# A hybrid decoder step on one core: the delta rule's norms as column scalars, and other first transfers

## The chip, the cores and the metric

The kernel runs on one core of a Trainium2 chip. A core has five engines that work at the same time and meet at semaphores: TensorE (PE: matmuls and transposes into PSUM; its weight loads are shown apart, as PEld), VectorE (DVE), ScalarE (ACT), GpSimd (POOL) and SyncE (SP), which here issues nearly all DMA transfers. Each engine takes its instructions strictly in the order in which they stand. The metric is the device time of one execution, in microseconds (us); lower is better.

## The reference, cut to what matters

One layer for 512 prompt rows and 8 x 4 sample rows of width 1024. Both kinds are modulated by a condition, multiplied by one wide projection (11280 columns), and go through two branches, windowed attention and a gated delta rule, which are merged at the end. The change touches the delta rule of the prompt rows (8 heads, head width 128):

```python
q = l2norm(q) * (B_HEAD_DIM ** -0.5)
k = l2norm(k)                                  # l2norm(t) = t * rsqrt(sum(t*t) + 1e-6)
...
cum = jnp.cumsum(g, axis=-1)
decay = jnp.exp(jnp.where(causal, cum[..., :, None] - cum[..., None, :], -jnp.inf))
kk = jnp.einsum('bhid,bhjd->bhij', k, k)
lower = jnp.where(strict, beta[..., :, None] * kk * decay, 0.0) + jnp.eye(n)
rhs = jnp.concatenate([beta[..., None] * v, beta[..., None] * k * jnp.exp(cum)[..., None]], axis=-1)
sol = lax.linalg.triangular_solve(lower, rhs, left_side=True, lower=True, unit_diagonal=True)
u, w = sol[..., :B_HEAD_DIM], sol[..., B_HEAD_DIM:]
v_new = u - jnp.einsum('bhid,bhde->bhie', w, state)
qk = jnp.einsum('bhid,bhjd->bhij', q, k) * decay
out = (q * exp(cum)) @ state + qk @ v_new
new_state = exp(cum[-1]) * state + (k * exp(cum[-1] - cum)).T @ v_new
...
ob = ob * lax.rsqrt(jnp.mean(ob * ob, axis=-1, keepdims=True) + NORM_EPS)   # after the rule, per row
```

It also returns the caches of keys and values, moved on by four rows (`kv*_s`, copied from input to output).

## The kernel before, in words

The kernel is written as a Python program that records operations, and a planner on the host, a list scheduler with rough costs for each engine, orders them before anything runs. All recorded operations are issued from one line of the program (L745 of the profile, L748 after the change), so the profile tells them apart by their tiles. What sets the order around the change: the order in which the code records, ranks, the earliest time `at` that a transfer may be planned, the costs in `Recorder.cost`, and the table `NUDGES`, which shifts margins in stretches of operations by seeded random numbers. Where the planner sees TensorE without work it puts in a placeholder, a matmul of ones (`warm<-ones`).

The front. `cT` (the conditions) and `bT` come in; `cs` is their silu. For each of the eight row tiles k: a block `wm[k]` of 1 MB is multiplied with `cs` (`pd<-wm,cs`), ScalarE copies the sum to `Y`, a product with the selection `selc` puts scale and shift into columns (`pd<-cst,Y`), VectorE applies them to `xT[k]`, and ScalarE and VectorE split the result into two rounded parts `hhi` and `hlo`; the weights `wf[k]` of the first three column tiles are split likewise (`whi`, `wlo`). The products of these three (`pp`, `pg`, `pb<-hhi,whi` and so on) run tile by tile behind it. `cst` is a block of constants (identity, `selc`, masks).

The stream. Then come 85 column tiles (`stream`, one `Job` each): 512 KB of weights (`wt`), split into `hi` and `lo`, three rounded products each, in two halves of 272 columns, in one of two PSUM banks (`pp`). ScalarE empties a bank (for the delta branch into `ext` and `cx`, the short convolution follows as `acc`). Between these products the planner lays the small work of attention and of the delta rule.

The delta rule of one head, `delta_blocks(h)` and, for two heads at once, `delta_rule(p)`. For four chunks of 128 rows: `NTs` is the decay, `cr` the exponent of the running sum as a row on all partitions, `rc` a tile of columns with one number a row of the chunk; `rc[:, 0]` becomes the reciprocal norm of k, `rc[:, 1]` that of q (times the scale). Before the change the norms are also needed along the free dimension: `rc` is transposed on TensorE (`pb<-cst,rc`), copied (`rrow`), written to DRAM (`dr`) and read back as two tiles `rb` with the same row on all partitions, and `QKd`, `NTs` and `cr` are multiplied with them. `NTs` then holds the lower matrix, `QKd` the products of q and k, `kr` the rows of k, `vr` those of v. Diagonal blocks of `NTs` go through DRAM (`dblk`) to `Ls`, are inverted into `Tb`, and go through `dtz` to `Tc`. `S` is the state, `vn` the new values, `z` the right side less the state's part.

The copies of the caches are 168 transfers of 496 or 512 KB from DRAM to DRAM (`moves`), which the planner may place at times spread evenly from 48 to 850 us.

Of the kernel before, what the change touches and what calls it, by code (L numbers as in the profile page):

```python
# [37 lines left out]
MOVES = (48.0, 850.0)  # L38
# [231 lines left out]
class Recorder:  # L270
# [103 lines left out]
    def cost(self, op, args):  # L374
# [23 lines left out]
        elif e == "ve":  # L398
# [8 lines left out]
            if op.name == "scalar_tensor_tensor" and pointer or op.name == "transpose":  # L407
                c += 0.055
            op.cost, op.late = c - 0.08, 0.08
        elif e == "se":  # L410
            c = (0.155 if in_psum else 0.21) + 0.83e-3 * n
            a = (0.07 if "accum_out" in op.kw else 0.0) + (0.08 if pointer else 0.0)
# [385 lines left out]
def body(ctx, tc, io):  # L798
# [27 lines left out]
    def pb_():  # L826
        return psb.tile([128, 512], F32, name="pb", tag="b")
# [67 lines left out]
    with ExitStack() as fctx:  # L895
        fr = pool(fctx, "front", 1)
        cT = fr.tile([128, KT, 9], F32, name="cT")
        sp.dma_start(cT, io["cT"])
        bT = fr.tile([128, 24], F32, name="bT")
        se.dma_start(bT, io["bT"])  # L900
# [11 lines left out]
        for k in range(KT):  # L912
            sp.dma_start(wm[k], io["w_mod"][k])
            if k == 0:
                sp.dma_start(cst, io["const"])
# [3 lines left out]
        rec.front = False  # L919
        sp.dma_start(wab, io["w_ab"])  # L920
# [9 lines left out]
        for k in range(KT):  # L930
# [3 lines left out]
            with rec.together():  # L934
                for i in range(KT):
                    q = i % 4
                    pe.matmul(pc[32 * q:32 * q + 32, 0:256], cs[:, i, :], wm[k][:, i, :], start=(i < 4), stop=(i >= 4),
                              tile_position=(0, 32 * q))
# [3 lines left out]
            for u in range(2):  # L942
                pe.matmul(pv[:, u, 0:9], Y[:, 128 * u:128 * u + 128], C("selc"), start=True, stop=True)
# [10 lines left out]
            ve.tensor_scalar(h[:, :SEQ], h[:, :SEQ], m[:, 1, 0:1], m[:, 0, 0:1], op0=OP.mult, op1=OP.add)  # L954
# [1491 lines left out]
```

## Time and profile before

| | us |
|---|---|
| median of three runs | 890.68 (887.01 to 891.37) |
| the profiled execution | 890.4 |
| its span in the profile | 888.6 |
| TensorE (PE) busy | 871.0 (98%) |
| VectorE (DVE) busy | 714.8 (80%) |
| ScalarE (ACT) busy | 431.8 (49%) |
| DMA, mean over the span | 272 GB/s |

The span is the time from the first instruction to the last; the execution's own time is 1.8 us longer. Busy means that an instruction is recorded on the engine; a placeholder of TensorE counts as busy, and matmuls that run at a lower clock do as well. The clock of TensorE that was granted is given as a share of its full speed. A row of the profile names the written tile, an arrow, and the tiles read, with buffer numbers left out.

### The profile page before, as it was taken

The numbers are of one execution on the slowest core, as the hardware profiler recorded it, in microseconds if no ns is written. First come the engines' busy times: TensorE is split into PE (matmuls) and PEld (weight loads), VectorE is DVE, ScalarE is ACT, GpSimd is POOL, SyncE is SP. The second block draws the span as 40 slices with busy tenths as digits, with TensorE's granted clock in tenths as the row PEclk, the third lists the DMA queues.
The fourth block names the chain that finished last, engine by engine and source line by source line (L and its number), as shares of the span: only waits on it lengthen the run. The fifth ranks groups of instructions, "written<-read, shape, count | busy, mean of one in ns | idle before, by whom it ended". The sixth has DMA issues, their size and how long they took to land.

```text
span 888.6 us, 20372 instructions
## 1 busy us (share of the span) xinstructions
PE 871.0 (98%) x7868; PEld 825.9 (93%) x7868; DVE 714.8 (80%) x1599; ACT 431.8 (49%) x1059; POOL 40.7 (5%) x115
## 2 busy tenths in 40 slices
PE   8999999999999998999999999999999999999996
PEld 7899999999998998997999999999999999997876
DVE  2678657777759989998999999777889889957657
ACT  2476645685544765444784644564531223234431
POOL 0030000010000000001000000011010000000000
PEclk8999999999999999999999999999999999999998
DMA  9786676557787788899687889479899999989983
GB/s 354 291 222 204 212 225 222 189 169 226 227 267 237 234 245 256 279 306 317 210 261 261 268 266 299 160 234 422 267 292 364 355 357 417 416 257 322 324 324 126
DMA packets 105796, 241.74 MB, mean 272 GB/s; under 512 B 32138, under 2 KB 59228, under 8 KB 101988
## 3 DMA queue, kind: packets, MB, share of 16 engines
q1 hardware_dynamic: 105556, 240.43, 80.2%
q8 instruction: 62, 1.02, 0.4%
q14 instruction: 34, 0.28, 0.1%
q10 hardware_dynamic: 144, 0.01, 0.0%
HBM read 223.79 MB, written 104.29 MB: 369 GB/s over the span
## 4 chain that ended last, share of the span: by engine, by line
PE 87%; DVE 4%; ACT 4%; DMA 2%; issue 1%; SPq 1%; POOL 1%; DVEq 0%; ACTq 0%; POOLq 0%
PE pp L745 65%; PE pg L745 9%; PE pd L745 9%; PE pb L745 3%; ACT L745 1%; DMA wm<-in_w_mod 1%; DMA wv<-dw 1%; DVE acc L745 1%; SPq L745 1%; DVE ya L745 1%; PE warm L745 0%; DVE NB L745 0%; ACT ext L745 0%; DVE XF L745 0%; POOL q L745 0%
## 5 line engine op out<-in xcount | busy, mean ns | idle before, releaser
L745 PE MATMUL pp<-hhi,hi 128*128 128x272 f32 x1360 | 399.5, 294 | 3.2 <-ACT cx L745 2.7
L745 PE MATMUL pp<-hlo,hi 128*128 128x272 f32 x1360 | 399.9, 294 | 0.0
L745 PE MATMUL pp<-hhi,lo 128*128 128x272 f32 x1360 | 399.5, 294 | 0.0
L745 PEld LDWEIGHTS pp<-hhi,hi 128*128 128x128 f32 x1360 | 257.1, 189 | 4.4 <-ACT cx L745 2.9
L745 PEld LDWEIGHTS pp<-hlo,hi 128*128 128x128 f32 x1360 | 257.4, 189 | 2.2 <-issue 1.4
L745 PEld LDWEIGHTS pp<-hhi,lo 128*128 128x128 f32 x1360 | 256.8, 189 | 1.5 <-issue 0.8
L745 ACT ACTIVATE hi<-wt 128x1024 fp32r<-128x1024 f32 (+1 forms) x101 | 103.6, 1026 | 166.3 <-PE pp L745 138.6
L745 DVE TENSOR_TENSOR lo<-wt,hi 128x1024 fp32r<-128x1024 f32 (+1 forms) x101 | 118.8, 1176 | 34.5 <-ACT hi L745 34.2
L745 DVE SCALAR_TENSOR_TENSOR acc<-ext,cw,acc 128x568 f32<-128x568 f32 x72 | 57.2, 801 | 5.9 <-ACT acc L745 5.4
L745 ACT ACTIVATE P<-P,st 128x256 f32<-128x256 f32 (+1 forms) x64 | 31.3, 491 | 34.5 <-DVE st L745 34.2
L745 DVE TENSOR_TENSOR slab<-slab 128x512 f32<-128x512 f32 (+1 forms) x66 | 42.9, 666 | 0.0
L745 DVE TENSOR_REDUCE slab<-slab 128x8 f32<-128x512 f32 (+2 forms) x66 | 42.4, 653 | 0.2
L745 ACT ACT_TABLE_LOAD x32 | 41.1, 1283 | 1.8 <-PEq L2419 1.2
L745 ACT ACTIVATE zt<-pp 128x272 f32<-128x272 f32 x48 | 18.7, 389 | 38.8 <-PE pp L745 33.4
L745 PE MATMUL pp<-ybh,hi 128*128 128x272 f32 x128 | 36.9, 288 | 0.0
L745 PE MATMUL pp<-ybh,lo 128*128 128x272 f32 x128 | 36.9, 288 | 0.0
L745 PE MATMUL pp<-ybl,hi 128*128 128x272 f32 x128 | 36.8, 288 | 0.0
L745 ACT ACTIVATE q<-pp 64x272 f32<-64x272 f32 (+1 forms) x48 | 26.2, 545 | 17.4 <-PE pp L745 16.9
L745 PE MATMUL pg<-k,q 128*128 128x128 f32 (+1 forms) x192 | 33.7, 307 | 0.4 <-DVE PT L745 0.4
L745 PEld LDWEIGHTS pg<-k,q 128*128 128x128 f32 x192 | 27.6, 190 | 2.8 <-issue 1.1
L745 DVE TENSOR_TENSOR tmp<-Ls,Tb 32x15 f32<-32x15 f32 (+7 forms) x120 | 23.1, 193 | 7.5 <-DMA Ls<-dblk 3.3
L745 DVE CUSTOM_DVE_ANT_0 P<-pg,bias 128x256 f32<-128x256 f32 (+1 forms) x64 | 24.0, 401 | 5.0 <-PE pg L745 4.5
(404 smaller groups left out, 1571.5 us busy)
## 6 DMA issues: line engine op xcount, KB each, us to landing
out_kv_s<-in_cache SPq DMA_DIRECT2D x144, 512.0 KB
wt<-in_w_in SPq DMA_DIRECT2D x85, 512.0 KB
out_kv_s<-in_cache SPq DMA_DIRECT2D x24, 496.0 KB
wm<-in_w_mod SPq DMA_DIRECT2D x8, 1024.0 KB
slab<-in_ks SPq DMA_DIRECT2D x32, 256.0 KB
slab<-in_vs SPq DMA_DIRECT2D x32, 256.0 KB
kv<-in_ks SPq DMA_DIRECT2D x16, 512.0 KB
kv<-in_vs SPq DMA_DIRECT2D x16, 512.0 KB
```

The costliest lines, as they stand in the source:

```text
L745: getattr(real[x.engine], x.name)(*map(arg, x.args), **{k: arg(v) for k, v in x.kw.items()})
```

## The change

The matrix of the triangular system and the products are brought to another basis by a diagonal matrix of k's norms. What was a factor on rows and on columns becomes a factor on rows alone, which is a column of scalars and needs no broadcast along the free dimension. `vr` is scaled by half the norm (`rc[:, 5]`, a second square root), `vn` by `beta` over the norm, and the outputs by q's reciprocal norm where ScalarE reads them. The transpose, `rrow`, `dr`, `rb` and the three multiplications go.

At the front `cT`, `bT` and `selc` come in one transfer `c0`; the first weights come in two halves, multiplied in two groups; `cst` comes behind the front; the first scaling of `xT` is done in two halves; and the weights of column tile 5, which were planned at time 0, are planned from 28 us on (`BEHIND`) as those of tiles 3 and 4 are. The cache copies are placed at times that reach 78% by 600 us, 95% by 800 and the last by 850. Two costs of the planner are altered, and `NUDGES` has other numbers.

```diff
-MOVES = (48.0, 850.0)
+MOVES = (48.0, 600.0, 800.0, 850.0), (0, 0.78, 0.95, 1)
...
 NUDGES = (
-    (0, 9912, 1047), (572, 972, 696727), (6242, 7442, 352100), (4626, 5026, 884219), (8230, 9430, 221759),
+    (0, 9881, 1023), (3823, 5023, 22586), (5072, 6272, 796932), (9467, 9507, 754021), (7424, 7824, 95492),
...
@@ cost
+            far = lambda v: v.ix.ndim > 1 and v.ix.shape[-1] > 1 and abs(int(v.ix.reshape(v.ix.shape[0], -1)[0, 1]) - int(v.ix.flat[0])) > 4
+            if n > 64 and any(far(v) for v in views if size(v) > 1):
+                c += 0.72e-3 * n
...
-            a = (0.07 if "accum_out" in op.kw else 0.0) + (0.08 if pointer else 0.0)
+            a = (0.015 if "accum_out" in op.kw else 0.0) + (0.08 if pointer else 0.0)
...
@@ front
-        cT = fr.tile([128, KT, 9], F32, name="cT")
-        sp.dma_start(cT, io["cT"])
-        bT = fr.tile([128, 24], F32, name="bT")
-        se.dma_start(bT, io["bT"])
+        c0 = fr.tile([128, 72 + 24 + 9], F32, name="c0")
+        sp.dma_start(c0, io["c0"])
+        cT, bT, selc = c0[:, 0:72].rearrange("p (k b) -> p k b", b=9), c0[:, 72:96], c0[:, 96:105]
...
         for k in range(KT):
-            sp.dma_start(wm[k], io["w_mod"][k])
-            if k == 0:
-                sp.dma_start(cst, io["const"])
+            for i in range(0, KT, KT if k else 4):
+                j = slice(i, KT if k else i + 4)
+                sp.dma_start(wm[k][:, j], io["w_mod"][k][:, j])
...
         rec.front = False
+        sp.dma_start(cst, io["const"])
...
-            with rec.together():
-                for i in range(KT):
-                    q = i % 4
-                    pe.matmul(pc[32 * q:32 * q + 32, 0:256], cs[:, i, :], wm[k][:, i, :], start=(i < 4), stop=(i >= 4),
-                              tile_position=(0, 32 * q))
+            for j in range(0, KT, KT if k else 4):
+                with rec.together():
+                    for i in range(j, KT if k else j + 4):
+                        q = i % 4
+                        pe.matmul(pc[32 * q:32 * q + 32, 0:256], cs[:, i, :], wm[k][:, i, :], start=(i < 4), stop=(i >= 4),
+                                  tile_position=(0, 32 * q))
...
-                pe.matmul(pv[:, u, 0:9], Y[:, 128 * u:128 * u + 128], C("selc"), start=True, stop=True)
+                pe.matmul(pv[:, u, 0:9], Y[:, 128 * u:128 * u + 128], selc, start=True, stop=True)
...
-            ve.tensor_scalar(h[:, :SEQ], h[:, :SEQ], m[:, 1, 0:1], m[:, 0, 0:1], op0=OP.mult, op1=OP.add)
+            for w in (slice(0, HF), slice(HF, SEQ)) if k == 0 else [slice(0, SEQ)]:
+                ve.tensor_scalar(h[:, w], h[:, w], m[:, 1, 0:1], m[:, 0, 0:1], op0=OP.mult, op1=OP.add)
...
@@ stream
-                    jobs[x].load(raws[x]).at = 0.0 if i else BEHIND
+                    jobs[x].load(raws[x]).at = 0.0 if i > 2 else BEHIND
...
@@ delta_blocks
-        rc = dl.tile([128, 5, 4], F32, name="rc")
+        rc = dl.tile([128, 6, 4], F32, name="rc")
...
+        se.activation(rc[:, 5], rc[:, 0], AF.Sqrt, bias=eps1[:, 0:1], scale=0.25)
         se.activation(rcf[:, 0:8], rcf[:, 0:8], AF.Sqrt, bias=eps4[:, 0:1])
         ve.reciprocal(rcf[:, 0:8], rcf[:, 0:8])
         ve.tensor_scalar(rc[:, 1], rc[:, 1], qscale, None, op0=OP.mult)
-        pn = pb_()
-        pe.transpose(pn[0:8, 0:128], rcf[:, 0:8], ident)
-        rrow = dl.tile([8, 128], F32, name="rrow", bufs=1)
-        ve.tensor_copy(rrow, pn[0:8, 0:128])
-        dr = dram.tile([8, 128], F32, name=f"dr{h}")
-        sp.dma_start(dr, rrow)
-        rb = dl.tile([128, 4, 128], F32, name="rb0", tag="vr"), dl.tile([128, 4, 128], F32, name="rb", bufs=1)
-        for a in range(2):
-            sp.dma_start(rb[a].rearrange("p c i -> p (c i)"),
-                         dr[4 * a:4 * a + 4].rearrange("a b -> (a b)")[None, :].to_broadcast([128, 512]))
-        for i, t in ((2, beta), (3, necum), (4, tail)):
+        for i, t in ((3, beta), (4, tail)):
             ve.tensor_mul(rc[:, i], rc[:, 0], t[:, h:32:8])
+        ve.tensor_mul(rc[:, 2], rc[:, 0], rc[:, 3])
         yield 1.0
-        ve.tensor_mul(QKd, NTs, rb[1])
-        ve.tensor_mul(NTs, NTs, rb[0])
-        ve.tensor_mul(cr, cr, rb[1].rearrange("p c i -> p (c i)"))
...
+                ve.scalar_tensor_tensor(QKd[:, c, :], pkv[:, cc, 1, :], rc[:, 0, c:c + 1], NTs[:, c, :],
+                                        op0=OP.mult, op1=OP.mult)
                 ve.scalar_tensor_tensor(NTs[:, c, :], pkv[:, cc, 0, :], rc[:, 2, c:c + 1], NTs[:, c, :],
                                         op0=OP.mult, op1=OP.mult)
-                ve.scalar_tensor_tensor(QKd[:, c, :], pkv[:, cc, 1, :], rc[:, 0, c:c + 1], QKd[:, c, :],
-                                        op0=OP.mult, op1=OP.mult)
-            yield 3.0 if c2 else 14.0
+            yield 3.0
...
-        se.activation(vr, cols128(pt), AF.Copy, scale=0.5)
+        for c in range(4):
+            se.activation(vr[:, c], cols128(pt)[:, c], AF.Copy, scale=rc[:, 5, c:c + 1])
...
@@ delta_rule
-                    ve.scalar_tensor_tensor(z, px[u][:, 0:128], rc[u][:, 3, c:c + 1], r[u], op0=OP.mult, op1=OP.add)
+                    col = c * 8 + hs[u]
+                    ve.scalar_tensor_tensor(z, px[u][:, 0:128], necum[:, col:col + 1], r[u], op0=OP.mult, op1=OP.add)
...
-                se.activation(vn[u], px[u][:, 128:256], AF.Copy, scale=beta[:, col:col + 1])
+                se.activation(vn[u], px[u][:, 128:256], AF.Copy, scale=rc[u][:, 3, c:c + 1])
...
-                se.activation(vr[u][:, c], px[u][:, 384:512], AF.Square, accum_out=rn[u][:, c:c + 1])
-                se.activation(vr[u][:, c], px[u][:, 384:512], AF.Copy)
+                rq = rc[u][:, 1, c:c + 1]
+                se.activation(vr[u][:, c], px[u][:, 384:512], AF.Square, scale=rq, accum_out=rn[u][:, c:c + 1])
+                se.activation(vr[u][:, c], px[u][:, 384:512], AF.Copy, scale=rq)
```

How the order moves on SP, at the start of the program, before (`wt` are a column tile's weights, `wm` the modulation weights, `xT` the rows, `wf` the first tiles' weights):

```order
L745 DMA wt<-in_w_in 128x1024
L745 DMA cT<-in_cT 128x72
L745 DMA wm<-in_w_mod 128x2048
L745 DMA cst<-in_const 128x298
L745 DMA xT<-in_xT 128x544
L745 DMA wf<-in_w_first 128x384
L745 DMA wm<-in_w_mod 128x2048
```

The same place after:

```order
L748 DMA c_94<-in_c 128x105
L748 DMA wm<-in_w_mod 128x1024 x2
L748 DMA xT<-in_xT 128x544
L748 DMA wf<-in_w_first 128x384
L748 DMA wm<-in_w_mod 128x2048
```

`wt` and `cst` no longer stand ahead of the second `wm`. On TensorE the front begins before with (`pd<-cst,Y` is the product with `selc`, `pp<-hhi,whi` the first product of the projection):

```order
L745 MATMUL warm<-ones 128x128 x15
L745 MATMUL pd<-wm,cs 32x256 x8
L745 MATMUL warm<-ones 128x128 x2
L745 MATMUL pd<-cst,Y 128x9 x2
L745 MATMUL warm<-ones 128x128 x7
L745 MATMUL pd<-wm,cs 32x256 x8
L745 MATMUL pp<-hhi,whi 128x272 x2
```

and after with:

```order
L748 MATMUL warm<-ones 128x128 x9
L748 MATMUL pd<-wm,cs 32x256 x4
L748 MATMUL warm<-ones 128x128
L748 MATMUL pd<-wm,cs 32x256 x4
L748 MATMUL warm<-ones 128x128 x4
L748 MATMUL pd<-c_94,Y 128x9 x2
L748 MATMUL warm<-ones 128x128 x5
L748 MATMUL pd<-wm,cs 32x256 x8
L748 MATMUL pp<-hhi,whi 128x272 x2
```

There are 19 placeholders instead of 24 there, and the first product is cut in two. On VectorE, in the fifth head (of eight), before, among convolution steps (`acc`, `KQ`, `us`) of the column tiles:

```order
L745 SCALAR_TENSOR_TENSOR acc<-ext,cw,acc 128x568
L745 TENSOR_TENSOR QKd<-NTs,rb 128x512
L745 SCALAR_TENSOR_TENSOR acc<-ext,cw,acc 128x568
L745 TENSOR_TENSOR NTs<-NTs,rb_4528 128x512
L745 SCALAR_TENSOR_TENSOR acc<-ext,cw,acc 128x568
L745 TENSOR_TENSOR cr<-cr,rb 128x512
L745 TENSOR_TENSOR lo<-wt,hi 128x1024
L745 SCALAR_TENSOR_TENSOR KQ<-ext,acc 128x4x128
```

and after, in one head of the same pair:

```order
L748 RECIPROCAL rc<-rc 128x8
L748 SCALAR_TENSOR_TENSOR acc<-ext,cw,acc 128x568
L748 TENSOR_SCALAR rc<-rc 128x4
L748 TENSOR_TENSOR rc<-rc,beta 128x4
L748 TENSOR_TENSOR rc<-rc,tail 128x4
L748 SCALAR_TENSOR_TENSOR QKd<-pb,rc,NTs 128x128
L748 TENSOR_TENSOR rc<-rc 128x4
L748 SCALAR_TENSOR_TENSOR QKd<-pb,rc,NTs 128x128
L748 SCALAR_TENSOR_TENSOR NTs<-pb,rc,NTs 128x128 x2
```

Nothing between the reciprocal and the products with `pb` comes from a transfer any more. On ScalarE, the two roots of one head now stand apart (`rc<-rc,small` are square roots, `P<-P,st` exponentials, `PT` an evacuation of attention):

```order
L748 ACT_TABLE_LOAD
L748 ACTIVATE rc<-rc,small 128x4
L748 ACTIVATE acc<-ext,cw 128x568
L748 ACTIVATE ext<-pp 128x272
L748 ACTIVATE PT<-pg 128x384
L748 ACT_TABLE_LOAD
L748 ACTIVATE P,st<-P,st 128x256 x2
```

where before only one stood there for a head, between two loads or with the next head's:

```order
L745 ACTIVATE rc<-rc,small 128x8
L745 ACT_TABLE_LOAD
L745 ACTIVATE ext<-acc 128x568
L745 ACTIVATE ext<-pp 128x240
L745 ACTIVATE ext<-pp 128x8x4
```

In all there are 42 loads of a table in the new order and 32 in the old.

More of the change, by code (lines that the diff above doesn't have):

```diff
@@ L1040, in body @@
         d = mv.dma_start(io[f"kv{g}_s"][b, r0:r1], io[f"cache{g}"][b, r0 + 4:r1 + 4])
-        d.at = MOVES[0] + (MOVES[1] - MOVES[0]) * i / len(moves)
+        d.at = float(np.interp(i / len(moves), MOVES[1], MOVES[0]))
     rec.rank = 0
@@ L1415, in delta_rule @@
                 pe.matmul(px[u][:, 128:256], XF2[:, u, c, :], r[u], start=True, stop=True)
-                col = c * 8 + hs[u]
-                se.activation(vn[u], px[u][:, 128:256], AF.Copy, scale=beta[:, col:col + 1])
+                se.activation(vn[u], px[u][:, 128:256], AF.Copy, scale=rc[u][:, 3, c:c + 1])
             yield 1.8
@@ L2383, in lay_out @@
         "xT": rows.T.reshape(KT, 128, NT).transpose(1, 0, 2),
-        "cT": c.T.reshape(KT, 128, 9).transpose(1, 0, 2),
+        "c0": np.concatenate([c.T.reshape(KT, 128, 9).transpose(1, 0, 2).reshape(128, 72), a["b_cond"][0].reshape(24, 128).T,
+                              np.arange(128)[:, None] % 32 == np.arange(9)], axis=1),
         "w_cond": a["w_cond"][0][:, 2 * D:],
@@ L2387, in lay_out @@
         "b_cond": a["b_cond"],
-        "bT": a["b_cond"][0].reshape(24, 128).T,
         "conv_w": a["conv_w"][0].T.reshape(24, 128, 4).transpose(1, 0, 2),
```

10 rows, old and new, of the table NUDGES are left out of this document.

## The prediction

> **What bounds the kernel now.** I read the profile's page first: busy times, and the 40 slices.
>
> ```profile
> span 888.6 us, 20372 instructions
> PE 871.0 (98%) x7868; PEld 825.9 (93%) x7868; DVE 714.8 (80%) x1599; ACT 431.8 (49%) x1059; POOL 40.7 (5%) x115
> ```
>
> TensorE is the bound, and it is busy for all but 888.6 - 871.0 = 17.6 us. Work taken from VectorE, ScalarE or the DMAs is worth nothing by itself; it counts only where TensorE stood idle, or ran at a lower clock, because of it. So I asked which waits end TensorE's idle time (columns: waiting instruction, what released it, us in total, times, longest).
>
> ```profile
> PE pp L745 <- ACT cx L745: 2.7, 1, 2.7
> PE pd L745 <- DMA wm<-in_w_mod: 2.0, 1, 2.0
> ```
>
> These two are the largest, and the change touches both. The chain that ended last shows the second one at its start, and the end of the kernel (start us, length us).
>
> ```profile
> 1.64 7.64 DMA wm<-in_w_mod
> ...
> 9.41 1.30 PE pd L745 x16
> ...
> 12.52 3.19 PE warm L745 x14
> 15.71 1.62 PE pd L745 x16
> ...
> 20.22 1.00 PE pd L745 x16
> ...
> 24.12 1.00 PE pd L745 x16
> ...
> 862.58 18.27 PE pp L745 x125
> ```
>
> TensorE waits for the first modulation weights until 9.41, and fills the time to 15.71 with placeholder matmuls (`warm`), which count as busy. From there the stages follow at 24.12 - 20.22 = 3.9 us. After the last product (880.85) VectorE needs the other 7.8 us; the change does not touch that end. The rate of the transfers and the clock in four stretches (columns: window, its length, PE, PEld, DVE, ACT and POOL busy with counts, granted clock, DMA share, GB/s):
>
> ```profile
> 7.00:10.00 3.00, 1.03 (x16) 0.75 (x18) 0.00 (x0) 0.00 (x0) 0.00 (x0) 1.00 1.04 399
> 10.00:17.00 7.00, 7.00 (x50) 5.37 (x39) 2.93 (x8) 2.09 (x5) 0.00 (x0) 0.51 1.03 418
> 334.00:337.10 3.10, 0.44 (x5) 0.22 (x3) 2.69 (x4) 1.18 (x5) 0.00 (x0) 1.00 0.83 245
> 337.80:341.20 3.40, 3.40 (x17) 3.40 (x16) 3.40 (x9) 0.68 (x3) 0.64 (x2) 0.50 0.80 265
> ```
>
> Both idle stretches are followed by a stretch at half clock.
>
> **The change, part by part.**
>
> *First transfers.* The order puts 512 KB (`wt`) ahead of everything and 149 KB (`cst`) between the first weights and the next; both go behind the front, and the first 1024 KB come in two halves.
>
> ```profile
> wt<-in_w_in SPq DMA_DIRECT2D x85, 512.0 KB
> wm<-in_w_mod SPq DMA_DIRECT2D x8, 1024.0 KB
> cst<-in_const SPq DMA_DIRECT2D x1, 149.0 KB
> ```
>
> 661 KB (677 kB) less at 399 to 418 GB/s bring the second `wm` 1.6 to 1.7 us earlier. When it lands now no row says, since 14 placeholder passes stand ahead of its product until 15.71. I estimate it from the first: that one is released at 9.28 (1.64 + 7.64), and the next stage's bytes (`wm` again and its two small companions, about 1.5 MB by the sizes in the program) take 3.7 us at 410 GB/s: near 13.2. In the new order it lands near 11.6. Ahead of its product stand five placeholders (ten passes; fourteen took 3.19 us, so 2.3 us) behind the small product on `Y`, which itself needs the second half and, new on ScalarE, the conversion `whi` placed ahead of `Y`. That side is ready near 12.2. So the front gains 15.71 - 12.2 = 3.5 us. Bounds: the bytes alone, 1.6 us, less a longer cold clock (1.5 us below), gives 0; a product at 11.6 at full clock (1.00 instead of 1.62) gives 4.7. I take 3.5, nearest to the landing. Later stages keep it: TensorE needs 3.9 us for a stage, the transfers 3.7. The `wt` that goes back is the sixth column tile's, multiplied long after; `cst` is now first used after the front, and eight transfers of 1024 KB ahead of it end before that; the copy of `bT` and its transfer ride in `c0`. The split first scaling of `xT` and the two extra issues on SP cost nothing: TensorE does the second stage's product meanwhile.
>
> *The broadcast rows.* Per head the order loses one transpose on TensorE, one small copy and three multiplications on VectorE, and one small and two 256 KB transfers. Where they are waited for, the timelines of VectorE, ScalarE and TensorE show (start, length, operation, and in brackets the idle time before and what ended it):
>
> ```profile
> 329.90 0.81 DVE L745 SCALAR_TENSOR_TENSOR acc<-ext,cw,acc 128x568 f32<-128x568 f32 x1
> 334.41 0.69 DVE L745 TENSOR_TENSOR NTs<-NTs,rb 128x512 f32<-128x512 f32 x1 [3.71 <-DMA rb<-dr]
> 335.02 0.80 DVE L745 SCALAR_TENSOR_TENSOR acc<-ext,cw,acc 128x568 f32<-128x568 f32 x1
> 335.92 0.68 ACT L745 ACTIVATE ext<-acc 128x568 f32<-128x568 f32 x1 [3.55 <-DVE acc L745]
> 336.83 0.21 ACT L745 ACTIVATE cx<-pp 128x27 f32<-128x27 f32 x1
> 337.09 0.39 PE L745 MATMUL pp<-hhi,hi 128*128 128x272 f32 x1 [2.66 <-ACT cx L745]
> ```
>
> VectorE waits 3.71 us for the broadcast, in order; a convolution step stands behind it, ScalarE's `ext` behind that, and `cx`, which frees the accumulator, behind that. This is the largest idle time of TensorE after the front: 2.66 us. Then 3.4 us run at clock 0.50 (window above): half of them, 1.7 us, is lost at most, and I take 1.5. The wait cannot return, since the broadcast is gone: 2.7 + 1.5 = 4.2 us. Bounds: 0 if the next late transfer on VectorE (`ya`, which needs `wv`, a few rows on) takes its place, 4.2 if not. I take 4.2, because `ya` waits for nothing in this trace.
>
> [...]
>
> *TensorE's own work.* Eight transposes go:
>
> ```profile
> 498.65 0.29 PE L745 MATMUL pp<-hhi,hi 128*128 128x272 f32 x1
> 499.10 0.27 PE L745 MATMUL pb<-cst,rc 128*8 128x128 f32 x1 [0.17 <-ACT kq L745]
> 499.13 0.37 PE L745 MATMUL pp<-hlo,hi 128*128 128x272 f32 x1
> ```
>
> One costs between 0.1 us and the 0.48 - 0.12 = 0.36 us seen here from 498.65 to 499.13: 0.15, times 8, makes 1.2 us less. Against it, the new order breaks small matmuls into more pieces: without the transposes I count 197 changes of the array's shape before and 210 now. A change costs about 0.1 to 0.2 us, as behind a run of 32-row matmuls that ends at 53.14:
>
> ```profile
> 53.14 0.39 PE L745 MATMUL pp<-hhi,hi 128*128 128x272 f32 x1
> 53.37 0.29 PE L745 MATMUL pp<-hlo,hi 128*128 128x272 f32 x1
> 53.49 0.29 PE L745 MATMUL pp<-hhi,lo 128*128 128x272 f32 x1
> ```
>
> The first step takes 0.23 us and the next, as usual, 0.12. 13 x 0.15 = +2.0 us; bounds 1 and 3.
>
> *ScalarE.* `vr` is made in four pieces with a scale column instead of one, 64 results get a scale column, and the order holds 42 table loads instead of 32.
>
> ```profile
> L745 ACT ACT_TABLE_LOAD x32 | 41.1, 1283 | 1.8 <-PEq L2419 1.2
> L745 ACT ACTIVATE vr<-pb 128x512 f32<-128x512 f32 x8 | 4.8, 598 | 8.3 <-PE pb L745 4.7 <-DMA dblk<-NTs 3.5
> L745 ACT ACTIVATE vn<-pd,beta 128x128 f32<-128x128 f32 x32 | 10.7, 367 | 10.9 <-PE pd L745 10.7
> L745 ACT ACTIVATE vr<-pd 128x128 f32<-128x128 f32 x64 | 16.9, 277 | 7.0 <-DVE S L745 4.8 <-PE pd L745 1.4
> ACT hi L745 <- PE pp L745: 138.6, 62, 5.9
> ...
> 184.03 1.28 ACT L745 ACT_TABLE_LOAD   x1
> 185.32 0.30 ACT L745 ACTIVATE rn<-rn,small 128x4 f32<-128x4 f32 x1
> ```
>
> 32 x 0.367 - 4.8 = 6.9; 64 x (0.367 - 0.277) = 5.8; eight more small roots of 0.30, 2.4; 10 x 1.283 = 12.8: together 28 us, ScalarE to 52%. It mostly lies beside other work: ScalarE waits for TensorE 62 times, 138.6 / 62 = 2.2 us at a time. But a pair of loads around one root takes 2 x 1.28 + 0.3 = 2.9 us, 0.7 more than that slack, for five heads: at most 3.5 us of late evacuations, at least 0. I take 1.0: two accumulators stand ready for TensorE.
>
> *Same instructions, other operands.* `QKd`, `NTs` and `z` take another column or another tile at the same shape, and the similarity leaves the count of TensorE's products alone: nothing.
>
> *VectorE* loses 24 multiplications of 0.69 us (row of 334.41) and 8 small copies, over 16 us. It is 94 of 100 us busy from 300 to 400 (next fence), so waits there may shrink; I count nothing.
>
> *Cache copies.* They are due by 600 for 78% of them instead of 69% (552/802): 15 more of 512 KB ahead of 600. At 400 GB/s that is 20 us of DMA time in 550; the 16 broadcasts that go, 256 KB each by their shape, give 10 us back. I count 0 for it; the price of a mistake is in the rivals. Fewer copies after 600 gain nothing, since TensorE never waits there (PE busy 100 of 100):
>
> ```profile
> 300.00:400.00 100.00, 97.19 (x791) 95.44 (x790) 93.68 (x221) 55.46 (x139) 3.26 (x14) 0.98 0.87 273
> ...
> 600.00:700.00 100.00, 100.00 (x882) 98.03 (x881) 84.57 (x138) 36.01 (x68) 9.67 (x15) 1.00 0.97 345
> ```
>
> *Sum*: -3.5 - 4.2 - 1.2 + 2.0 + 1.0 = -5.9 us. It is made against the profiled execution: 890.4 us, its span of 888.6 and 1.8 around it, 0.3 below the median of 890.68 (runs from 887.0 to 891.4). That gives 884.5 us.
>
> **The rivals.**
>
> *Denser copies make a new wait (the other side).* VectorE works in order, so one late small transfer (`Ls`, `wv`, `Tc`, the row `cr`), queued behind several 512 KB copies, does what `rb` did: 3.7 us there, 2.7 idle and 1.5 of clock on TensorE, 4.2 us each. One brings 888.7, two 892.9; from two on the kernel is no faster. For it: the DMA share was already 0.87 from 300 to 400, and the new SP order has up to three copies in a row between such transfers. Against: in 168 copies before, it happened once, and to a transfer that is gone.
>
> *The front gains nothing.* Then 888.0. For it: fewer placeholders leave TensorE idle longer ahead of the first weights, and the clock may stay at half past 17 us, into the products. Against: 677 kB less have to arrive.
>
> *Other waits shrink too.* Of 17.6 - 7.8 = 9.8 us of idle time that is not the end, 5.1 are left by my terms; with VectorE 16 us lighter, most of it may go: 884.5 - 4 = 880.5.
>
> [...]
>
> [...]
>
> **How the numbers follow.** Forecast (881.5 to 887.5) 0.54; other waits shrink too 0.13; front gains nothing 0.09; one new wait 0.12; two or more 0.08; ScalarE the bound 0.04. A difference under 0.5% (4.45 us, so 886.2 to 895.1) cannot be told from none. Faster: 0.13 and nine tenths of 0.54, 0.62. Slower: three waits or more (897; 0.05 of the 0.08) and ScalarE, 0.09. The rest, 0.29, is the same. The range goes from 878.5 (front 4.7, and nearly all of the 5.1 us of other waits) to 890.5 (the front nothing, and half of a new wait): 0.12 lie above for two waits and ScalarE, and some 0.08 at its edges.
>
> **What would show it.** Right: TensorE's product on the second `wm` starts at 11.5 to 13; no `rb` among the waits; no gap of over 2 us of TensorE between 50 and 850; 42 table loads and no chain through them. Wrong: a half-clock stretch after 17 us; VectorE waiting over 3 us for `Ls`, `wv`, `Tc` or `cr`; TensorE waiting for ScalarE's `ext`, `cx` or `q` behind a table load.

## The result, and the profile after

The changed kernel takes 893.2 us (median of 9 runs, 892.5 to 896.6). Before, 9 runs have a median of 887.0 us (885.1 to 891.4). The ratio is 1.0066, with a 95% interval of 1.0049 to 1.0084: it is slower by 5.8 us, where 884.5 was forecast. The execution of before that the prediction read (890.4 us) was one of its longer ones, 3.4 us above this median; this matters below.

Heading and busy times of the page of after:

```profile
span 891.2 us, 20324 instructions
PE 871.3 (98%) x7850; PEld 820.4 (92%) x7850; DVE 702.0 (79%) x1568; ACT 454.8 (51%) x1101; POOL 40.9 (5%) x115
```

VectorE has lost 12.8 us of work and ScalarE has gained 23.0. TensorE's busy time is the same within 0.3 us, and its idle time has grown from 17.6 to 19.9 us, although the 2.7 us behind `cx` at 334 us are gone and the waits for `wm` have shrunk from 2.0 to 1.0. TensorE's waits after (waiting instruction, what released it, us in total, times, longest):

```profile
PE pp L748 <- DVE zt L748: 1.8, 2, 1.4
PE pb L748 <- ACT QKd L748: 1.6, 4, 0.6
...
PE pd L748 <- DMA wm<-in_w_mod: 1.0, 2, 0.9
PE pg L748 <- ACT P L748: 0.9, 3, 0.4
...
PE pb L748 <- ACT ext L748: 0.8, 1, 0.8
PE pd L748 <- ACT vr L748: 0.6, 1, 0.6
```

No single wait is as long as the 2.7 us of before (the longest is 1.4); there are many of 0.3 to 0.9, ended by ScalarE and VectorE. The second product on `wm` in TensorE's timeline:

```profile
10.86 1.07 PE L748 MATMUL pd<-wm,cs 128*32 128x256 f32 x16
```

And the clock there (window, its length, PE, PEld, DVE, ACT, POOL busy, granted clock, DMA share, GB/s):

```profile
10.00:17.00 7.00, 6.85 (x69) 5.20 (x68) 4.68 (x13) 3.22 (x7) 0.00 (x0) 1.00 1.04 417
```

It starts at 10.86 instead of 15.71, at clock 1.00 instead of 0.51. ScalarE's groups that answer to those of the prediction:

```profile
L748 ACT ACT_TABLE_LOAD x42 | 53.9, 1283 | 1.5 <-PEq L2415 0.7
L748 ACT ACTIVATE vr<-pd,rc 128x128 f32<-128x128 f32 x64 | 22.2, 368 | 4.6 <-DVE S L748 4.0
L748 ACT ACTIVATE vr<-pb,rc 128x128 f32<-128x128 f32 x32 | 9.9, 376 | 7.9 <-PE pb L748 5.5 <-DMA out_kv_s<-in_cache 2.4
```

The sizes are as forecast: 368 ns with the scale column, 42 loads. VectorE's longest waits for transfers:

```profile
DVE slab L748 <- DMA slab<-in_ks: 4.0, 3, 1.5
...
DVE lo L748 <- DMA x<-dv: 3.1, 1, 3.1
...
DVE ya L748 <- DMA wv<-dw: 2.4, 2, 1.4
DVE tmp L748 <- DMA Ls<-dblk: 1.8, 2, 1.5
```

There is no `rb`, and none of the named ones (`Ls`, `wv`, `Tc`, `cr`) is over 3 us. Of the four signs that the prediction had listed as "right", no `rb` and no gap of over 2 us are there. The product came early (10.86, not 11.5 to 13). The 42 loads are there, but the chain that ended last does run through loads: they are 18.4 us of it, 10.3 before (17.7 in after_again, 5.2 in before_again). Whether they cost anything is tested below.

### The profile page after: what moved, and what is told of

It is laid out like the page before. It is cut to its first block, busy times and chain, and to the rows that moved or that the text cites. A ratio compares the mean times of both kernels' runs of the same rounds, so it can differ in the third digit from the quotient of the medians.

```text
span 891.2 us, 20324 instructions
## 1 busy us (share of the span) xinstructions
PE 871.3 (98%) x7850; PEld 820.4 (92%) x7850; DVE 702.0 (79%) x1568; ACT 454.8 (51%) x1101; POOL 40.9 (5%) x115
## 4 chain that ended last, share of the span: by engine, by line
PE 70%; DMA 9%; ACT 9%; DVE 8%; issue 2%; SPq 1%; POOL 1%; DVEq 0%; POOLq 0%; ACTq 0%
PE pp L748 54%; PE pg L748 7%; PE pd L748 6%; PE pb L748 3%; ACT L748 2%; DVE slab L748 2%; DVE lo L748 2%; DMA wv<-dw 2%; DMA slab<-in_ks 1%; ACT hi L748 1%; ACT QKd L748 1%; DMA xT<-in_xT 1%; ACT vr L748 1%; DMA wf<-in_w_first 1%; DMA wm<-in_w_mod 1%
## 5 line engine op out<-in xcount | busy, mean ns | idle before, releaser
L748 ACT ACTIVATE spare<-pp 128x272 f32<-128x272 f32 (+1 forms) x32 | 16.1, 502 | 22.8 <-PE pp L748 22.8
```

The lines of the kernel that those rows point to most:

```text
L748: getattr(real[x.engine], x.name)(*map(arg, x.args), **{k: arg(v) for k, v in x.kw.items()})
```

## The experiments

A planner sets the order from costs and from a table of numbers, so undoing one part in the code would also reorder the rest. Therefore most kernels here carry an order that is written out: the list of instructions that the planner gave for before (or for after), and each edited instruction at the place of the one that it replaces:

```diff
-        rec.schedule()
+        rec.follow(PLAN)
```

"In the order of before" and "in the order of after" below mean this. With the same instruction sequence, two traces can be laid side by side, TensorE's n-th instruction against its n-th, and the lead of one over the other read at each.

| kernel | order of | median us | ratio to before, 95% |
|---|---|---|---|
| before_again | before | 886.9 | 0.9985 (0.9969 to 1.0002) |
| front_kept_order | before | 885.7 | 0.9982 (0.9966 to 0.9998) |
| delta_kept_order | before | 890.5 | 1.0031 (1.0017 to 1.0046) |
| both_kept_order | before | 891.8 | 1.0037 (1.0020 to 1.0054) |
| delta_vr_one_piece | before | 888.6 | 1.0011 (0.9997 to 1.0024) |
| delta_plain_out | before | 887.8 | 0.9997 (0.9983 to 1.0010) |
| both_mended | before | 890.9 | 1.0032 (1.0020 to 1.0044) |
| copies_denser_kept_order | before | 898.0 | 1.0122 (1.0103 to 1.0141) |
| after_copies_back | after | 901.0 | 1.0143 (1.0113 to 1.0173) |
| after_one_root | after | 900.9 | 1.0141 (1.0117 to 1.0165) |
| after_plain_out | after | 898.2 | 1.0110 (1.0083 to 1.0136) |
| front_rb_later | before | 884.6 | 0.9963 (0.9948 to 0.9978) |
| after_again | after | 893.8 | 1.0062 (1.0039 to 1.0085) |
| after_one_root2 | after | 893.5 | 1.0059 (1.0036 to 1.0081) |
| after_plain_out2 | after | 888.4 | 1.0006 (0.9989 to 1.0022) |
| both_plain_out | before | 886.8 | 0.9992 (0.9976 to 1.0008) |
| both_mended2 | before | 885.0 | 0.9977 (0.9963 to 0.9992) |
| front_rb_later2 | before | 884.4 | 0.9955 (0.9938 to 0.9971) |

One thousandth is 0.9 us. The runs were made in five groups, each on another chip beside runs of before, so kernels are compared by their ratios. before_again has the instructions of before and differs by 1.3 us, with an interval that reaches 1: a difference of that size alone shows nothing.

**before_again**: no edit but the written order.

> The kernel before, its order written out instead of planned: the same instructions in the same order. For a second profile of it. If the wait of 2.66 us at 334 us with the half clock behind it belongs to the kernel, it is there again and the time is 890; if it belonged to that one execution, the time is near 886.5 and there is no such gap.

The wait at 334 us is there again, but shorter, and without the half clock behind it (TensorE's timeline):

```profile
334.27 0.40 PE L969 MATMUL pp<-hhi,hi 128*128 128x272 f32 x1 [1.61 <-ACT cx L969]
```

TensorE's waits:

```profile
PE pd L969 <- DMA wm<-in_w_mod: 3.4, 2, 3.1
PE pp L969 <- ACT cx L969: 1.6, 1, 1.6
PE pd L969 <- issue: 1.4, 1, 1.4
```

And the window behind the wait:

```profile
334.30:337.70 3.40, 3.40 (x27) 3.40 (x28) 3.40 (x8) 1.60 (x4) 0.64 (x2) 1.00 1.02 351
```

So the wait belongs to the kernel, its 4.2 us did not: 1.6 us here, and 0.9 in front_kept_order, which leaves this place alone. The front has no half clock here (1.00 from 0 to 50 us).

**front_kept_order**: the hunks on `c0`, the split first product and scaling, the place of `cst` and `wt`.

> The kernel before with the new front alone (first transfers, split first product, c0). Behind the front every engine has the order of before, written out, not planned anew. Theory A (the parts of the change are worth what they seem, and the loss comes from the new order of the rest): the front's gain of about 4 us lasts to the end, 883 us against 887, ratio 0.995. Theory B (the delta rule's edits cost the time): the same here, 883. Theory C (the front's gain is given back whatever the order, since the next stage waits for something that did not move): 886 to 888, ratio 0.999 to 1.001.

It gains 1.6 us (0.2 to 3.0), between theories A and C. Second and last product on `wm`, before_again and then front_kept_order:

```profile
14.05 1.07 PE L969 MATMUL pd<-wm,cs 128*32 128x256 f32 x16 [0.32 <-DMA wm<-in_w_mod]
...
36.28 1.07 PE L969 MATMUL pd<-wm,cs 128*32 128x256 f32 x16
```

```profile
10.65 1.07 PE L969 MATMUL pd<-wm,cs 128*32 128x256 f32 x16
...
34.56 1.07 PE L969 MATMUL pd<-wm,cs 128*32 128x256 f32 x16 [0.94 <-DMA wm<-in_w_mod]
```

The lead is 3.4 us at the second stage and 1.7 at the eighth, where TensorE waits 0.94 us for the weights. At 48 us it is 1.4, and it stays within 1.4 to 1.7 until 260. The second stage is a poor mark, though: in the six profiles of the old front in this order it starts anywhere from 11.46 us (delta_kept_order) to 15.64 (before). The first product of the stream (`pp<-hhi,hi`) is steadier: it starts at 47.59 to 50.34 us in these six and at 46.26 to 47.51 in the seven of the new front in this order, 1.5 us apart in the median. The old front ran at clock 0.51 from 10 to 17 us in before and at 1.00 over the first 50 us in before_again and copies_denser_kept_order; the new one ran at 1.00 over the first 50 us in after. The gain is what 661 KB less take, 1.6 us at 410 GB/s. So it looks as if the transfers pace the whole front; the DMA share fits that (in after 1.04 from 10 to 17 us and 0.97 from 17 to 40), but no run tests it.

**delta_kept_order**: the hunks on the delta rule, each new instruction in the old one's place, the new root right ahead of the old one (32 table loads).

> The kernel before with the new delta rule alone (no broadcast rows, scale columns, vr in four pieces, the second root right ahead of the first), each new instruction at the place of the one that it replaces, all the rest in the order of before. Theory A: 8 transposes (-1.2 us) and 24 multiplications less, no rb to wait for: 884 to 887, ratio 0.996 to 1.000. Theory B (ScalarE's four vr pieces, scale columns and roots delay what TensorE waits for): 889 to 893, ratio 1.003 to 1.007.

Slower by 2.7 us, theory B, though the wait for `rb` is gone: laid against before_again, it has lost 3.1 us by 322 us in many small steps, the two largest (0.4) where TensorE enters `pb`, gets 2.6 back from 334 to 339, where the wait for `rb` was, and loses 2.4 again by 605.

**both_kept_order**: both.

> New front and new delta rule together, the rest in the order of before: the changed kernel without its new order, cache copy times and planner costs. Theory A: 880 to 883, ratio 0.993 to 0.996, so the changed kernel's 893 is lost to its order. Theory B: 886 to 890. Theory C: 884 to 887.

Slower by 3.3 us, beyond theory B's 890: the front's gain does not show here (the two parts alone add up to +1.1, with intervals that allow 3.3). Of the changed kernel's 5.8 us the edits themselves explain more than half; the intervals of the two (1.0020 to 1.0054 and 1.0049 to 1.0084) overlap.

**delta_vr_one_piece**: as delta_kept_order, with

```diff
-        for c in range(4):
-            se.activation(vr[:, c], cols128(pt)[:, c], AF.Copy, scale=rc[:, 5, c:c + 1])
+        se.activation(vr, cols128(pt), AF.Copy, scale=0.5)
```

This leaves the norm of the key out of `vr`.

> As the kernel with the new delta rule alone in the order of before (890.5 us, ratio 1.003), but vr is copied from the one pb accumulator in one piece with the constant 0.5, as before, instead of four pieces with a scale column. It leaves the norm of the key out of vr. Theory P (the four pieces, 1.49 us for 0.60, hold the only pb accumulator, and TensorE's next product into pb waits): 1.5 to 2.5 us faster, 888 to 889, ratio 1.000 to 1.0015, and TensorE's waits for vr fall from 1.4 to 0.2 us. Theory Q (the pieces are hidden; something else in the new delta rule costs): 890 to 891, ratio 1.003.

1.8 us faster than delta_kept_order (ratio 1.0011 for 1.0031; the intervals overlap, so the time alone does not settle it). TensorE's wait for `pb`, first with four pieces, then with one:

```profile
PE pb L969 <- ACT vr L969: 1.4, 4, 0.7
```

```profile
PE pb L968 <- ACT vr L968: 0.2, 1, 0.2
```

This is theory P's wait, 1.2 us less: there is one `pb` accumulator, and the four pieces, which overlap, keep ScalarE busy for 9.1 / 8 = 1.14 us a head instead of 0.60.

**delta_plain_out**: as delta_kept_order, with

```diff
-                se.activation(vr[u][:, c], px[u][:, 384:512], AF.Square, scale=rq, accum_out=rn[u][:, c:c + 1])
-                se.activation(vr[u][:, c], px[u][:, 384:512], AF.Copy, scale=rq)
+                se.activation(vr[u][:, c], px[u][:, 384:512], AF.Square, accum_out=rn[u][:, c:c + 1])
+                se.activation(vr[u][:, c], px[u][:, 384:512], AF.Copy)
```

This leaves the scale of the query out of the output.

> As the kernel with the new delta rule alone in the order of before, but the 64 evacuations vr<-pd (square and copy) have no scale column, 277 ns each instead of 367. It leaves the scale of the query out of the output. Theory Q1 (these 5.3 us of ScalarE delay the passes of the recurrence that wait for pd): 1 to 2 us faster, 888.5 to 889.5, ratio 1.001 to 1.002. Theory P: no change, 890 to 891, ratio 1.003.

Faster than delta_kept_order by 3.0 us (0.9997 for 1.0031, intervals apart), more than theory Q1 said. The evacuation with the column (delta_kept_order) and without it:

```profile
L969 ACT ACTIVATE vr<-pd,rc 128x128 f32<-128x128 f32 x64 | 22.2, 367 | 6.7 <-DVE S L969 4.8 <-PE pd L969 1.2
```

```profile
L969 ACT ACTIVATE vr<-pd 128x128 f32<-128x128 f32 x64 | 17.0, 278 | 7.0 <-DVE S L969 4.8 <-PE pd L969 1.4
```

And the idle time before instructions on `pd` that `vr` ended (us, times), in the same two kernels:

```profile
  ACT vr L969: 1.8, 7
```

```profile
  ACT vr L969: 0.3, 2
```

Nearly all of it lies before TensorE's weight loads for `pd<-S,KQ`: 1.5 us in six waits, then 0.3 in two.

**both_mended**: as both_kept_order, with

```diff
+        ve.tensor_scalar(rc[:, 5], rc[:, 0], 0.5, None, op0=OP.mult)
...
+        ve.tensor_mul(vr, cols128(pt), rc[:, 5, :, None].to_broadcast([128, 4, 128]))
```

in place of the second root and of the four pieces.

> New front and new delta rule in the order of before (891.8 us, ratio 1.004), with vr as one VectorE multiplication by the broadcast column, and the second root replaced by half of the first one (one small VectorE operation, no root). Full computation. Theory P: the pb accumulator is released 0.8 us earlier per head; 1.5 to 2.5 us faster than with both parts, 889 to 890, and if the front's 1.6 us also come through, 886 to 887, ratio 0.999 to 1.000. Theory Q: 891 to 892, since ScalarE was not what cost.

No gain (1.0032 for 1.0037). TensorE now waits for the same accumulator behind VectorE, which takes `vr` in its turn:

```profile
PE pb L969 <- DVE vr L969: 2.7, 5, 0.8
```

VectorE also waits here for the root in `rc`, 10.8 us in eight waits; what such a place costs is seen below in the order of after, and was not separated here.

**copies_denser_kept_order**: before, with the 168 cache copies issued at the due times of after.

> The kernel before with its order written out; only the 168 cache copies are issued at the places that the changed kernel's due times give them (78% by 600 us, 95% by 800), all else in the order of before. Theory D (the denser copies delay weights and small transfers, which makes the changed kernel slower): 889 to 891, ratio 1.002 to 1.004. Against it (my forecast's zero): 886.5 to 888, ratio 0.9985 to 1.0005.

10.8 us slower, far outside both. VectorE's wait for a small transfer, in before_again and then here:

```profile
DVE tmp L969 <- DMA Ls<-dblk: 3.5, 1, 3.5
```

```profile
DVE tmp L969 <- DMA Ls<-dblk: 10.5, 3, 4.4
```

What TensorE waits for here:

```profile
PE pg L969 <- DVE vrow L969: 3.3, 2, 3.0
PE pb L969 <- DVE QKd L969: 2.5, 4, 1.1
```

This is the prediction's first rival, a late small transfer at the head of VectorE's queue. TensorE's two waits are 4.8 us longer than in before_again (0 and 1.0 there); the rest of the 10.8 us is not traced to single instructions, so that `Ls` causes all of it is argued, not shown. In the changed kernel, whose order was planned around these copies, VectorE waits only 1.8 us for `Ls` (3.0 in after_again).

**after_copies_back**: after, with the copies at the due times of before.

> The changed kernel (893.2 us, ratio 1.0066) with its own order written out; only the 168 cache copies are issued where the due times of before put them (evenly from 48 to 850 us). Theory D (the denser copies cost here too, as they cost 10.8 us in the order of before): 889 to 891, ratio 1.002 to 1.004. Theory O (the new order was planned with the denser copies and hides them; with the old times its small transfers and weights fit worse or the same): 892 to 895, ratio 1.005 to 1.009.

7 us slower than after_again, more than theory O said. Now VectorE waits for other transfers; how much of the 7 us they make was not separated:

```profile
DVE lo L972 <- DMA out_conv_s<-crow: 5.9, 1, 5.9
DVE ya L972 <- DMA wv<-dw: 4.6, 2, 3.5
```

An order and the times of its copies go together: exchanging them costs 7 to 11 us either way.

**after_again**: after, with its order written out.

> The changed kernel with its own order written out instead of planned: the same instructions. If the order alone is what the time hangs on: 892.5 to 894 as before, ratio 1.005 to 1.0085.

893.8 us, as the planned one: the comparison for what follows.

**after_one_root, after_plain_out**: after, with half of the first root in place of the second, and after without the 64 scale columns, its scale put into the epsilon of the norm (`rc[:, 6]` is 128 eps / rq squared):

```diff
+        ve.scalar_tensor_tensor(rc[:, 6], rc[:, 1], 128 * NORM_EPS / qscale ** 2, rc[:, 1], op0=OP.mult, op1=OP.mult)
...
-            se.activation(rn[u], rn[u], AF.Sqrt, bias=eps1[:, 0:1], scale=1.0 / 128)
+            ge.tensor_add(rn[u], rn[u], rc[u][:, 6])
+            se.activation(rn[u], rn[u], AF.Sqrt, scale=1.0 / 128)
```

> The changed kernel with its own order written out; the root for the key's norm is replaced by half of the other root (one small VectorE operation per head), full computation. ScalarE then loads 32 tables instead of 42. Theory T (the ten loads of 1.28 us and the roots delay what TensorE waits for): 890 to 891.5, ratio 1.003 to 1.005. Theory H (the loads lie beside other work): 892 to 894, ratio 1.0055 to 1.0075.

> The changed kernel with its own order written out; the 64 evacuations vr<-pd have no scale column (277 ns each instead of 368), and the query's scale goes into the norm's epsilon instead: one small VectorE operation and one small GpSimd operation per head, full computation. Theory Q1 (the scale columns cost 2.7 us, as in the order of before): 889.5 to 891, ratio 1.003 to 1.0045. Theory O (in the new order they are hidden, and the order is what costs): 892.5 to 894, ratio 1.006 to 1.0075.

Both were slower than after, by 7 and 4 us, which no theory said. The cause is where I put the small VectorE operation: right behind the root, ahead of VectorE's other work. Timeline of after_one_root (in brackets the idle time before and what ended it):

```profile
317.24 1.28 ACT L972 ACT_TABLE_LOAD   x1
...
318.54 0.30 ACT L972 ACTIVATE rc<-rc,small 128x8 f32<-128x8 f32 x1
...
318.87 0.17 DVE L972 TENSOR_SCALAR rc<-rc 128x4 f32<-128x4 f32 x1 [1.95 <-ACT rc L972]
...
323.39 0.89 PE L972 MATMUL pb<-KQ 128*128 128x256 f32 x3 [1.85 <-DVE NTs L972]
```

VectorE waits 1.95 us for a table load and a root, the products with `pb` come later, and TensorE waits 1.85 us. In its waits, five of these make 5.4 us:

```profile
PE pb L972 <- DVE NTs L972: 5.4, 5, 1.8
```

**after_one_root2, after_plain_out2, both_plain_out**: the same edits with that operation right ahead of the reciprocal, which waits for the root anyway.

> The changed kernel in its own order with half of the first root instead of a second one, its small VectorE operation right ahead of the reciprocal: 32 table loads instead of 42, full computation. Theory T (the loads cost): 1.5 us or more faster than the changed kernel on this chip, near 891. Theory H (they lie beside other work): within 1 us of it. If the 4 to 8 us of the first try came from the place of the small operation, they are gone in either case.

893.5 against 893.8: theory H. Ten table loads and eight roots less, for eight small VectorE operations more, are worth nothing here.

> The changed kernel in its own order without the scale columns in the 64 evacuations vr<-pd, the scale in the norm's epsilon, its small VectorE operation right ahead of the reciprocal; full computation. Theory Q1: 2 to 3 us faster than the changed kernel on this chip, 890 to 891, ratio 1.003 to 1.0045. Theory O (hidden in this order): within 1 us of it.

888.4 against 893.8, or 5.0 us by the ratios (1.0006 for 1.0062): more than theory Q1 said, and nearly the whole loss of the changed kernel. Idle time before instructions on `pd` that `vr` ended, after_again and then after_plain_out2:

```profile
  ACT vr L972: 3.2, 10
```

```profile
  ACT vr L972: 1.6, 5
```

Of these, 2.2 us in eight waits and then 0.8 in three lie before TensorE's weight loads for `pd<-S,KQ` (the rest is a product behind such a load and one wait of VectorE), so 1.3 to 1.4 us can be pinned on single instructions. That all 5.0 us run through `pd` is argued, not shown. Laid side by side, the rest comes in steps of 0.1 to 0.5, most of them in the stretches with a recurrence (160 to 200, 420 to 440, 540 to 600 us), and in two steps of 1.2 to 1.3 at 536 and 608 us, at places where two executions of the same order also differ by 0.85.

> New front and new delta rule in the order of before (891.8 us, ratio 1.0037), without the scale columns in the 64 evacuations, the scale in the norm's epsilon; full computation. Theory Q1: 888 to 889.5, ratio 1.000 to 1.0015, and with the front's gain come through 886 to 887. Else 891 to 892.

886.8 us, 4.0 less than both_kept_order by the ratios (0.9992 for 1.0037, intervals apart): Q1 again, and more than it said.

**front_rb_later, front_rb_later2**: front_kept_order, with one of VectorE's multiplications by `rb` moved behind the convolution step and four operations that stood behind it.

> The new front alone in the order of before (885.7 us, ratio 0.998), and in one head the multiplication NTs by rb is put behind the convolution step and the four short operations that stood behind it, so that VectorE does not wait there for the broadcast (334 us in the profile). The delta rule is that of before. If that wait costs about 2.4 us as the two traces say: 883 to 884.5, ratio 0.995 to 0.997. If the wait only moves to the next instruction that needs rb: 885.5 to 886.5, ratio 0.998.

> The new front alone with one rb multiplication moved, again (884.6 us, ratio 0.996), on the same chip as the kernel with both parts mended. 884 to 885, ratio 0.9955 to 0.997.

884.6 and 884.4, 1.7 and 2.4 us less than front_kept_order by the ratios, with intervals that overlap. At that wait both traces gain 1.1 us on front_kept_order, which waited 0.9 there, and 1.8 on before_again, which waited 1.6. No wait for `rb` is left on VectorE: it did not move on.

**both_mended2**: both_plain_out, with `vr` copied in one piece and scaled on GpSimd:

```diff
-        for c in range(4):
-            se.activation(vr[:, c], cols128(pt)[:, c], AF.Copy, scale=rc[:, 5, c:c + 1])
+        se.activation(vr, cols128(pt), AF.Copy)
+        ge.tensor_mul(vr, vr, rc[:, 5, :, None].to_broadcast([128, 4, 128]))
```

> New front and new delta rule in the order of before, without the scale columns in the 64 evacuations (scale in the norm's epsilon), and vr copied from pb in one piece as before and scaled by the norm on GpSimd (one multiplication of 128x512 per head); full computation. If the four pieces cost 1.8 us here as they did alone: 885, ratio 0.997. If GpSimd's operation makes VectorE or the inverse wait: 887 to 889, ratio 1.000 or above.

885.0, as expected: freed of both costs on ScalarE, the changed kernel in this order is 5.3 us faster than both_kept_order and 2.0 us (0.7 to 3.3) faster than before. The front alone gave 1.6 of that, so a gain of the new delta rule itself is not shown. front_rb_later (0.9955 and 0.9963) has the lowest times: the new front, the old delta rule, one instruction moved; on the same chip it is 0.5 us below both_mended2, which does not tell them apart.

## Why the prediction was wrong, point by point

- *First transfers, -3.5.* Measured -1.6: the bound "the bytes alone, 1.6 us" was the value. The forecast time of the second product on `wm`, 12.2, was not too early (10.86; the landing estimate ahead of it has a slip, 9.28 + 3.7 is 13.0 and not 13.2, which does not enter the 12.2). What failed is the time that it was taken from: 15.71 was that one execution's, with TensorE at half clock from 10.12 to 16.95, and in five other profiles the same front gets there at 11.46 to 14.07. Nor did "later stages keep it" hold in the pair of traces: six stages take 3.98 us each in front_kept_order and 3.71 in before_again.
- *The `rb` wait, -4.2.* The mechanism was right: VectorE in order, then `ext`, `cx`, TensorE. The term was mis-sized. Moving that one instruction gave 1.7 and 2.4 us; TensorE waited 1.6 us in before_again, with clock 1.00 behind it, and 0.9 in front_kept_order. The sum had taken one long execution for the typical one. The base has the same fault: 890.4 less 5.9 is 884.5, but 887.0 less 5.9 would have been 881.1.
- *Transposes and shapes of the array, +0.8 net.* The changes of shape in the trace of after are 216, with 219 before, 16 of them at the transposes: the count of 13 more elsewhere was right. Their time was not measured by itself.
- *ScalarE, +1.0.* This is the step that decided. The added work was counted fairly (28 us; ScalarE rose by 23), but not where it lies. I divided the 138.6 us that ScalarE waits before `hi` by 62 and took 2.2 us of slack for every instruction, and I had said that two accumulators stand ready. That holds for `pp`. The 64 evacuations read `pd`, inside a recurrence in which each pass needs both `pd` accumulators back: their scale columns, 5.2 us of ScalarE's busy time (22.2 for 17.0), cost 3.0, 4.0 and 5.0 us in three comparisons. The four pieces of `vr` hold `pb`, of which there is one: 1.8 and 1.3 us in two comparisons, neither clear of noise alone. Both together cost 5.3 us in the order of before (both_kept_order and both_mended2), for a forecast of 1.0. And the table loads, to which I gave the whole 1.0, cost nothing that after_one_root2 shows, though the chain that ended last runs through more of them than before. The scale column itself took 367 - 278 = 89 ns an evacuation (delta_kept_order and delta_plain_out).
- *VectorE, 0.* 12.8 us less work (16 were forecast). No run takes this part alone.
- *Cache copies, 0.* Wrong as a reason, since the same copies cost 10.8 us in the other order. What they cost in the changed kernel's own order no run tells, since moving them back made a misfit of the other sign.
- *The rivals.* The 0.04 for ScalarE as the bound named the right engine. No run shows it held behind a table load: in before the load at 184.03 us ends at 185.31, and the next instruction starts at 185.32. What the runs show is the 3.0 to 5.0 us of the scale columns. "Other waits shrink too" failed: TensorE's idle time grew. "The front gains nothing" was too low by the 1.6 us. A new VectorE wait that holds TensorE did not appear in the changed kernel: the one over 3 us (`lo` for `x<-dv`) has no wait of TensorE of its length, and is under 1 us in after_again.

Both parts in the order of before give +3.3 us and the changed kernel +5.8. What the other 2.5 us are (new numbers, planner costs, denser copies) was not separated; their interval reaches zero. Without the scale columns the two orders are 1.2 us apart (after_plain_out2 and both_plain_out), with overlapping intervals.

## What to carry to other kernels

Price added work on an engine at the buffer that it holds: how many copies of that buffer there are, and whether a chain of dependent products needs it back. An average of the engine's idle time says nothing about that. At the front here, the gain was no more than the time of the bytes that were removed. And before a wait, a start time or a base goes into a sum, see whether a second execution has it at that size.

## What the runs showed of the hardware that was not expected

Runs of 32x32 products sometimes stop in the middle with no releaser in the trace ("issue"), and not alike in every profile of the same order: 1.42 us at 419 in before_again, 1.60 us at 558 in both_kept_order, and 0.3 us in all on `pd` in delta_plain_out. The one in both_kept_order and the window behind it:

```profile
558.26 0.18 PE L969 MATMUL pd<-W,XF 32*32 32x32 f32 x1 [1.60 <-issue]
```

```profile
559.10:562.40 3.30, 3.30 (x36) 1.94 (x25) 1.57 (x4) 0.70 (x3) 0.00 (x0) 0.50 0.89 323
```

The 3.30 us of that window ran at clock 0.50. A gap of 1.61 us cost no clock in before_again (1.00 in the window from 334.30 above), nor did one of 2.01 in after_plain_out2:

```profile
607.63 0.39 PE L972 MATMUL pp<-hhi,hi 128*128 128x272 f32 x1 [2.01 <-DVE zt L972]
```

```profile
607.70:611.00 3.30, 3.30 (x48) 3.13 (x52) 3.09 (x5) 0.00 (x0) 1.16 (x3) 1.00 1.03 405
```

Half clock also followed gaps of 2.66 us in before (0.50 from 337.80 to 341.21) and 2.25 in after_plain_out (0.50 from 612.6 to 615.9). copies_denser_kept_order has gaps of 2.97 at 403 and 1.67 at 418, and its clock is 0.98 over the 100 us from 400 to 500: that is room for one stretch of about 3.4 us, not for two. In before the stretch behind the gap is 3.41 us long, and the one in the front, from 10.12 to 16.95, 6.83.

So the length of a gap does not decide by itself; what does, no run shows. The wait at 334 us had clock 0.50 behind it in before, where it took 2.66 us, and 1.00 in before_again, where it took 1.61.
